# A hybrid decoder layer: a branch's results kept in SBUF, block sums on another engine and at other steps, stores and reloads traced later

## The chip, the cores and the metric

The kernel runs on one core of a Trainium2 chip. The metric is the device time of one execution in microseconds (us). The engines are PE (matrix products; PEld its weight loads), DVE (vector), ACT (scalar), POOL (GpSimd) and SP, whose queue issues nearly all DMAs here. Each engine works through its own queue in order.

## The reference

One layer with two token mixers on the same normalised input, for a prompt of 1040 tokens (16 learned meta tokens and 1024 of the sequence) and for 8 sample tokens. All of it is float32.

```python
proj = rmsnorm(h, norm_pre) @ w_in                   # 1024 -> 10 x 1024
q, fr, i_in, z_a, b_g, c_g, h_c, z_b, gate_a, gate_b = split(proj)
o = gated_linear_recurrence(silu(q), 1 - f, i_in, log f)   # 8 heads, 128x128 state
y_a = (norm(o) * silu(z_a)) @ w_a                    # branch A
u = c_g * h_c
y_b = (b_g * causal_conv3(u) * silu(z_b)) @ w_b      # branch B
merged = sigmoid(gate_a) * y_a + sigmoid(gate_b) * y_b
h = h + rmsnorm(merged @ w_o, norm_post)
```

It also returns the new recurrent states and the last two rows of u.

## The kernel before

**The products.** Tokens lie along the free dimension (1032 columns of a 128-row block), channels along partitions. A float32 product is made from three: both factors are split into a high and a low part, and `mm3` (L112) adds high x high, high x low and low x high. On top of that lies a Strassen scheme with seven products j = 0 to 6: `strassen` (L556) runs a list of *streams*, each a pair of 128-column blocks of weights against seven precomputed factors `s0` to `s6` of the right side (tiles `s0h`, `s0l` and so on). A stream has 14 *steps*, for each j two chunks of some 256 columns, 12 matmuls a step. There are 47 streams, numbered here from 0: 0 to 21 belong to the heads of branch A (with seven of the eight gate streams among them), 22 to 37 to the convolution (`u_pair` L670 and `b_pair` L730 in turn for 8 blocks), 38 to the last gate pair, 39 to 42 to y_a (`w_a`), 43 to 46 to y_b (`w_b`). In the windows below stream 38 starts at 990.60 us, 39 at 1019.60, 42 at 1094.10 and 45 at 1164.40; the windows are cut at the first product of a stream.

**The order.** The program is written out by hand (`manual_schedule`): an engine executes its instructions in the order in which the Python code issues ("traces") them. In each step `strassen` traces PE's 12 matmuls, then what was put off (`flush`: copies and evacuations of the step before), then the high part (ACT, L605) or the low part (DVE, L611) of the weights two products ahead, then whatever `at_step` (L861) has hung on that step's number. `add` (L587) forms two sums of weights for the next stream on POOL (L591 to L593), `low` a further one (L615). Held products are copied out of PSUM by ACT (L570); PE adds the next product onto the same bank, so it waits for that copy. Raw weights arrive in five slots `wq` by `load_quarter` (L93), four loads a stream.

**Between the branches.** The right side of y_a and y_b is the output of the recurrence (`oz_d`) or of the convolution (`ob_d`), kept in DRAM as 8 blocks of 128 x 1032. The seven factors need block sums: `block_sums(k, ...)` (L842) loads blocks k and k+4 into slots `f` and `k`, forms four differences of 128x516 in `s`, `f` and `k`, and stores them in `ta` or `tb` (three stores). The tags are slots of SBUF; a slot's new user waits until the last one is done. Branch A's four calls come out of `sample_steps` (L786), which computes the sample tokens of a head in 11 parts beside the convolution and is woven into 154 steps from step 350 on; branch B's four calls are hung on steps A0+6 to A0+36 (A0 = 546 is the first step of y_a, B0 = 602 that of y_b).

`exchange` (L864) replaces the factors while the products of the stream before still use the old ones: 14 units, one per half factor, each two loads of 258 KB into a raw slot, an ACT copy of 128x1032 (L90) and a subtraction of the same size (L91), on POOL for every third unit and on DVE for the others. Units are hung on steps A0-13 to A0+8 and B0-13 to B0+8, one every 1.65 steps. Branch A rotates through six raw slots, branch B through five; the reload of a slot is traced right behind the unit that frees it.

**The results.** The gates wait in DRAM (`ga_d`, `gb_d`). `gates_in` loads two blocks of them into `x` and `zs`; `y_pair` (L909) multiplies the product into the gate's slot; branch A's products are then stored in DRAM (`md`, L920), and in branch B `merged_in` loads them again (L906) to be added. After the streams the merged blocks are split and multiplied by `w_o`.

Of the kernel before, what the change touches and what calls it, by code (L numbers as in the profile page):

```python
# [19 lines left out]
HL = 524  # L20
HY = 516
# [11 lines left out]
def hybrid_step(ctx: ExitStack, tc: tile.TileContext,  # L33
# [728 lines left out]
    def context_out():  # L762
        for g in range(2):
            pt = hbank()
            for j in range(4):
                c = NEW + 18 * (4 * g + j)
                pe.transpose(pt[0:18, 128 * j:128 * j + 128], cx[:, c:c + 18], ident)
            nct = slot(("f", "s")[g], 512)
            act.copy(nct[0:18], pt[0:18])
            sync.dma_start(conv_p_out[0, 0][:, 512 * g:512 * g + 512], nct[0:2])  # L770
            sync.dma_start(conv_s_out[0].rearrange("b j d -> (b j) d")[:, 512 * g:512 * g + 512], nct[2:18])
# [13 lines left out]
    def sample_steps():  # L785
        loaded = sample_state(0)  # L786
        for m in range(8):
# [43 lines left out]
            if m >= 4:  # L831
                yield from block_sums(m - 4, oz_d, *sums_a)
# [9 lines left out]
    def block_sums(k, src, t12, t34):  # L842
        up, low, t = slot("f", NY), slot("k", NY), slot("s", NY)
        sync.dma_start(up, src[k])
        sync.dma_start(low, src[k + 4])
        yield
        yield
        less(t[:, L], up[:, R], up[:, L], pool)
        less(t[:, R], low[:, R], t[:, L], pool)
        yield  # L850
        sync.dma_start(t12[k], t)
        less(up[:, R], low[:, R], up[:, R], pool)
        less(low[:, L], low[:, L], t[:, R], pool)
        yield
        sync.dma_start(t34[k][:, L], up[:, R])
        sync.dma_start(t34[k][:, R], low[:, L])
        yield
# [3 lines left out]
    def at_step(g, f):  # L861
        hooks.setdefault(g, []).append(f)

    def exchange(g0, g1, base, sets, src, t12, t34, tags):  # L864


        of = lambda j, k: (src[k][:, L], src[k + 4][:, L], t12[k][:, R], t12[k][:, L], t34[k][:, L], t34[k][:, R],
                           src[k + 4][:, R])[j]
        raw = {}

        def load_unit(v):
            if v < 14:
                j, i = divmod(v, 2)
                raw[v] = slot(tags[v % len(tags)], NY)
                for q in range(2):
                    sync.dma_start(raw[v][:, HY * q:HY * q + HY], of(j, 2 * i + q))

        def unit(v):
            j, i = divmod(v, 2)
            if not i:  # L880
                sets[j] = factor(j)
            here = [[HL, 2], [1, HY]]
            split(raw[v].rearrange("p (q c) -> p q c", q=2), cap(sets[j][0], 2 * HL * i, here),
                  cap(sets[j][1], 2 * HL * i, here), pool if v % 3 == 2 else vec)
            load_unit(v + len(tags))

        for v in range(len(tags)):
            at_step(g0 + int(g1 * v), lambda v=v: load_unit(v))
        for v in range(14):
            at_step(base + 1 + int(1.65 * v), lambda v=v: unit(v))  # L890


    md = spilled("md")
    gated_ = {}
    merged = {}
    MERGED = ("v", "a", "ee", "s", "it", "u", "kt", "f")

    def gates_in(src, m):
        for r, tag in ((0, "x"), (1, "zs")):
            gated_[src is gb_d, m + r] = g = slot(tag, NY)  # L900
            sync.dma_start(g, src[m + r])

    def merged_in(m):
        for r in range(2):
            merged[m + r] = slot(MERGED[m + r], NY)
            sync.dma_start(merged[m + r], md[m + r])  # L906

    def y_pair(w, m, sets, second):
        def evac(r, h, c0, n, pt, s):  # L909
            ys = slice(HY * h + c0, HY * h + c0 + n)  # L910
            g = gated_[second, m + r][:, ys]
            vec.tensor_tensor(out=g, in0=added(pt, s), in1=g, op=ALU.mult)  # L912
            if second:
                t = merged[m + r][:, ys]
                vec.tensor_tensor(out=t, in0=t, in1=g, op=ALU.add)

        def end():
            if not second:
                for r in range(2):
                    sync.dma_start(md[m + r], gated_[second, m + r])  # L920

        return (w[0][:, 128 * m:128 * m + 128], w[0][:, 128 * m + 128:128 * m + 256]), chunks_of(HY), (), evac, end, sets
# [45 lines left out]
    exchange(A0 - 20, 1, A0 - 14, sets_a, oz_d, *sums_a, ("it", "u", "v", "a", "ee", "kt"))  # L968
    exchange(B0 - 20, 1, B0 - 14, sets_b, ob_d, *sums_b, ("it", "u", "kt", "f", "k"))
    at_step(A0 + 2, lambda: context_out())  # L970
    b_sums = (x for k in range(4) for x in block_sums(k, ob_d, *sums_b))
    for i in range(24):
        at_step(A0 + 6 + int(1.25 * i), lambda: next(b_sums, None))
    for i, m in enumerate((0, 2, 4, 6)):
        at_step(A0 - 11 + 14 * i, lambda m=m: gates_in(ga_d, m))
        at_step(B0 - 11 + 14 * i, lambda m=m: gates_in(gb_d, m))
        at_step(B0 - 8 + 14 * i, lambda m=m: merged_in(m))
# [199 lines left out]
    weave(stream, 14 * 11, sample_steps(), [1] * (8 * N_SAMPLE + 4 * 5))  # L1177
# [10 lines left out]
    wpost = slot("k", 1024)  # L1188
# [42 lines left out]
    xt, y, yl, ms = slot("v", 1024), slot("w", 1024), slot("a", 1024), small(2)  # L1231
# [50 lines left out]
```

## Time and profile before

| | |
|---|---|
| median of 3 runs | 1313.02 us (1312.26 to 1315.84) |
| the profiled execution | 1310.55 us, its span 1308.8 us |
| mean granted clock of PE | 0.989 |
| busy: PE, DVE, ACT, POOL | 1243.9, 940.0, 578.3, 504.7 us |
| moved by DMA | 148.85 MB |

Busy time is the sum of an engine's instructions; an engine that waits or issues DMAs is not busy. PEclk is the share of PE's full clock (2.4 GHz) that was granted in a stretch, its lower level 1.2 GHz. A row of waits says which engine's line waited for whom, how long in total, how often and the longest time. In a timeline, the brackets hold the idle time before an instruction and what ended it.

### The profile page before, as it was taken

The numbers are of one execution on the slowest core, as the hardware profiler recorded it, in microseconds if no ns is written. First come the engines' busy times: TensorE is split into PE (matmuls) and PEld (weight loads), VectorE is DVE, ScalarE is ACT, GpSimd is POOL, SyncE is SP. The second block draws the span as 40 slices with busy tenths as digits, with TensorE's granted clock in tenths as the row PEclk, the third lists the DMA queues.
The fourth block names the chain that finished last, engine by engine and source line by source line (L and its number), as shares of the span: only waits on it lengthen the run. The fifth ranks groups of instructions, "written<-read, shape, count | busy, mean of one in ns | idle before, by whom it ended". The sixth has DMA issues, their size and how long they took to land. (4 is left out here: it accounts for less than half of the span.)

```text
span 1308.8 us, 25416 instructions
## 1 busy us (share of the span) xinstructions
PE 1243.9 (95%) x9849; PEld 1203.7 (92%) x9849; DVE 940.0 (72%) x1520; ACT 578.3 (44%) x1364; POOL 504.7 (39%) x534
## 2 busy tenths in 40 slices
PE   6899999999999999999999999998998979899997
PEld 5799999999999999999999999898998979899876
DVE  5779596786959677695976788566865848979252
ACT  5455555455555545555443333333335514436031
POOL 5735242422423243242423444655744555520010
PEclk9899999999999999999999999999999989999999
DMA  6011212121121212112114354554337589753141
GB/s 221 9 46 55 61 57 82 59 74 59 58 67 55 82 55 75 58 58 68 55 60 139 106 146 114 162 168 126 113 115 266 197 278 357 255 200 125 49 163 56
DMA packets 162502, 148.85 MB, mean 114 GB/s; under 512 B 10353, under 2 KB 134362, under 8 KB 162382
## 3 DMA queue, kind: packets, MB, share of 16 engines
q1 hardware_dynamic: 161806, 145.14, 34.7%
q8 instruction: 77, 1.26, 0.4%
q0 software_dynamic: 576, 2.10, 0.4%
q14 instruction: 43, 0.35, 0.1%
HBM read 108.50 MB, written 38.67 MB: 112 GB/s over the span
## 5 line engine op out<-in xcount | busy, mean ns | idle before, releaser
L611 DVE TENSOR_TENSOR w<-wq,w 128x512 fp32r<-128x512 f32 x185 | 162.5, 878 | 66.3 <-ACT w L605 65.2
L605 ACT CAST w<-sm 128x512 fp32r<-128x512 f32 x141 | 87.3, 619 | 208.5 <-PE gb L116 134.0
L611 DVE TENSOR_TENSOR w<-sm,w 128x512 fp32r<-128x512 f32 x141 | 112.4, 797 | 48.7 <-ACT w L605 48.2
L591 POOL TENSOR_TENSOR sm<-wq 128x512 f32<-128x512 f32 x47 | 79.0, 1680 | 172.3 <-DVE w L611 153.8
L570 ACT COPY sc<-ga 128x256 f32<-128x256 f32 x216 | 80.1, 372 | 124.6 <-PE ga L116 104.9
L615 POOL TENSOR_TENSOR sm<-wq,sm 128x512 f32<-128x512 f32 x47 | 71.6, 1523 | 155.4 <-DVE w L611 112.9
L605 ACT CAST w<-wq 128x512 fp32r<-128x512 f32 x188 | 116.7, 622 | 29.4 <-PE ga L116 21.4
L114 PE MATMUL gb<-s1h,w 128*128 128x256 f32 (+3 forms) x376 | 109.0, 290 | 2.0 <-DVE sc L696 1.8
L114 PE MATMUL gb<-s3h,w 128*128 128x256 f32 (+3 forms) x376 | 109.2, 291 | 1.6 <-ACT w L605 1.1
L116 PE MATMUL gb<-s3h,w 128*128 128x256 f32 (+3 forms) x376 | 107.4, 286 | 3.2 <-DVE w L611 3.1
L114 PE MATMUL gb<-s6h,w 128*128 128x256 f32 (+3 forms) x376 | 108.3, 288 | 2.3 <-DVE f L288 1.5
L116 PE MATMUL gb<-s1h,w 128*128 128x256 f32 (+3 forms) x376 | 106.3, 283 | 2.8 <-DVE w L611 2.8
L115 PE MATMUL gb<-s3l,w 128*128 128x256 f32 (+3 forms) x376 | 107.0, 285 | 0.0
L115 PE MATMUL gb<-s6l,w 128*128 128x256 f32 (+3 forms) x376 | 106.5, 283 | 0.0
L115 PE MATMUL gb<-s1l,w 128*128 128x256 f32 (+3 forms) x376 | 106.2, 282 | 0.0
L116 PE MATMUL gb<-s6h,w 128*128 128x256 f32 (+3 forms) x376 | 106.0, 282 | 0.0
L288 DVE TENSOR_TENSOR sc<-gb,sc 128x256 f32<-128x256 f32 x192 | 80.5, 420 | 35.2 <-ACT sc L570 18.1
L593 POOL TENSOR_TENSOR sm<-wq 128x512 f32<-128x512 f32 x47 | 65.3, 1389 | 74.6 <-DVE w L611 73.5
L114 PE MATMUL ga<-s5h,w 128*128 128x256 f32 (+3 forms) x288 | 85.3, 296 | 8.5 <-ACT sc L570 8.0
L114 PE MATMUL ga<-s0h,w 128*128 128x256 f32 (+3 forms) x288 | 83.1, 288 | 1.1 <-DVE zs L327 1.1
L114 PE MATMUL ga<-s2h,w 128*128 128x256 f32 (+3 forms) x288 | 84.1, 292 | 0.0
L115 PE MATMUL ga<-s5l,w 128*128 128x256 f32 (+3 forms) x288 | 83.3, 289 | 0.4 <-DVE s5l L200 0.4
(677 smaller groups left out, 4487.8 us busy)
## 6 DMA issues: line engine op xcount, KB each, us to landing
wq<-in_w_in_dram SPq DMA_DIRECT2D x160, 256.0 KB
oz<-zs SPq DMA_DIRECT2D x16, 258.0 KB
ob<-zs SPq DMA_DIRECT2D x8, 516.0 KB
wq<-in_w_a_dram SPq DMA_DIRECT2D x16, 256.0 KB
wq<-in_w_b_dram SPq DMA_DIRECT2D x16, 256.0 KB
wq<-in_w_o_dram SPq DMA_DIRECT2D x16, 256.0 KB
wq<-in_x_prompt_dram SPq DMA_DIRECT2D x16, 256.0 KB
out_dram<-w SPq DMA_DIRECT2D x16, 256.0 KB
```

The lines of the kernel that those rows point to most:

```text
L114: pe.matmul(pt, wh, xh, start=first, stop=False, skip_group_check=onto)
L115: pe.matmul(pt, wh, xl, start=False, stop=False, skip_group_check=onto)
L116: pe.matmul(pt, wl, xh, start=False, stop=last, skip_group_check=onto)
L288: vec.tensor_tensor(out=out, in0=pt, in1=s, op=ALU.add)
L570: act.copy(held[j][:, cols], o)
L591: pool.tensor_tensor(out=s3, in0=a11, in1=a21, op=ALU.subtract)
L593: pool.tensor_tensor(out=s2, in0=a21, in1=a11, op=ALU.subtract)
L605: act.copy(w[:, 0:512], source(i))
L611: (pool if j in pairs[p][2] else vec).tensor_tensor(out=w[:, 512:1024], in0=source(i), in1=w[:, 0:512].bitcast(F32), op=ALU.subtract)
L615: pool.tensor_tensor(out=s2, in0=raws[p, 0, 1], in1=s2, op=ALU.subtract)
```

## The change

Branch A's gates are loaded into the eight slots that will hold the merged blocks, `ee`, `f`, `s`, `k`, `v`, `a`, `it`, `u`, and the product stays there; `md`, its eight stores and its eight reloads are gone. Branch B's gates use `x` and `zs`. With fewer free slots, exchange A has five raw slots (`it`, `u`, `v`, `a`, `kt`) and exchange B three (`kt`, `x`, `zs`), and a reload is traced two steps behind the unit that frees its slot.

`block_sums` runs on DVE, one subtraction a step, the first three steps after the loads are traced, and its stores come a step or two after what they store. All eight calls are hung on steps: branch A's at 435, 450, 465 and 480, branch B's at 494, 505, 516 and 541 (A0-5). The first seven lie beside the convolution (streams 31 to 37), the eighth in stream 38. `sample_steps` no longer calls them, and its 88 parts are woven into 126 steps in place of 108 into 154. The last rows of the convolution leave from `x` and `zs`, eight steps later, and three later loads use other slots.

```diff
@@ -765,7 +765,7 @@
             for j in range(4):
                 c = NEW + 18 * (4 * g + j)
                 pe.transpose(pt[0:18, 128 * j:128 * j + 128], cx[:, c:c + 18], ident)
-            nct = slot(("f", "s")[g], 512)
+            nct = slot(("x", "zs")[g], 512)
             act.copy(nct[0:18], pt[0:18])
             sync.dma_start(conv_p_out[0, 0][:, 512 * g:512 * g + 512], nct[0:2])
             sync.dma_start(conv_s_out[0].rearrange("b j d -> (b j) d")[:, 512 * g:512 * g + 512], nct[2:18])
@@ -828,8 +828,6 @@
             sync.dma_start(oz_d[m][:].rearrange("p (h c) -> p h c", h=2)[:, :, 512:516],
                            smpz[:, 8 * m:8 * m + 8].rearrange("p (h c) -> p h c", h=2))
             yield
-            if m >= 4:
-                yield from block_sums(m - 4, oz_d, *sums_a)
 
 
 
@@ -839,18 +837,22 @@
     sums_a, sums_b = sums_of("ta"), sums_of("tb")
     L, R = slice(0, HY), slice(HY, NY)
 
-    def block_sums(k, src, t12, t34):
-        up, low, t = slot("f", NY), slot("k", NY), slot("s", NY)
+    def block_sums(k, src, t12, t34, tags):
+        up, low, t = (slot(tag, NY) for tag in tags)
         sync.dma_start(up, src[k])
         sync.dma_start(low, src[k + 4])
         yield
         yield
-        less(t[:, L], up[:, R], up[:, L], pool)
-        less(t[:, R], low[:, R], t[:, L], pool)
-        yield
+        yield
+        less(t[:, L], up[:, R], up[:, L], vec)
+        yield
+        less(t[:, R], low[:, R], t[:, L], vec)
+        yield
+        less(up[:, R], low[:, R], up[:, R], vec)
+        yield
+        less(low[:, L], low[:, L], t[:, R], vec)
         sync.dma_start(t12[k], t)
-        less(up[:, R], low[:, R], up[:, R], pool)
-        less(low[:, L], low[:, L], t[:, R], pool)
+        yield
         yield
         sync.dma_start(t34[k][:, L], up[:, R])
         sync.dma_start(t34[k][:, R], low[:, L])
@@ -861,65 +863,57 @@
     def at_step(g, f):
         hooks.setdefault(g, []).append(f)
 
-    def exchange(g0, g1, base, sets, src, t12, t34, tags):
+    def exchange(g0, base, sets, src, t12, t34, tags):
 
 
         of = lambda j, k: (src[k][:, L], src[k + 4][:, L], t12[k][:, R], t12[k][:, L], t34[k][:, L], t34[k][:, R],
                            src[k + 4][:, R])[j]
-        raw = {}
+        raw = []
 
         def load_unit(v):
-            if v < 14:
-                j, i = divmod(v, 2)
-                raw[v] = slot(tags[v % len(tags)], NY)
-                for q in range(2):
-                    sync.dma_start(raw[v][:, HY * q:HY * q + HY], of(j, 2 * i + q))
+            j, i = divmod(v, 2)
+            if v < len(tags):
+                raw.append(slot(tags[v], NY))
+            for q in range(2):
+                sync.dma_start(raw[v % len(tags)][:, HY * q:HY * q + HY], of(j, 2 * i + q))
 
         def unit(v):
             j, i = divmod(v, 2)
             if not i:
                 sets[j] = factor(j)
             here = [[HL, 2], [1, HY]]
-            split(raw[v].rearrange("p (q c) -> p q c", q=2), cap(sets[j][0], 2 * HL * i, here),
+            split(raw[v % len(tags)].rearrange("p (q c) -> p q c", q=2), cap(sets[j][0], 2 * HL * i, here),
                   cap(sets[j][1], 2 * HL * i, here), pool if v % 3 == 2 else vec)
-            load_unit(v + len(tags))
-
-        for v in range(len(tags)):
-            at_step(g0 + int(g1 * v), lambda v=v: load_unit(v))
+
+        when = lambda v: base + 1 + int(1.65 * v)
         for v in range(14):
-            at_step(base + 1 + int(1.65 * v), lambda v=v: unit(v))
-
-
-    md = spilled("md")
-    gated_ = {}
-    merged = {}
-    MERGED = ("v", "a", "ee", "s", "it", "u", "kt", "f")
-
-    def gates_in(src, m):
-        for r, tag in ((0, "x"), (1, "zs")):
-            gated_[src is gb_d, m + r] = g = slot(tag, NY)
-            sync.dma_start(g, src[m + r])
-
-    def merged_in(m):
-        for r in range(2):
-            merged[m + r] = slot(MERGED[m + r], NY)
-            sync.dma_start(merged[m + r], md[m + r])
+            at_step(g0 + v if v < len(tags) else when(v - len(tags)) + 2, lambda v=v: load_unit(v))
+            at_step(when(v), lambda v=v: unit(v))
+
+
+    merged, gates_b = {}, {}
+    MERGED = ("ee", "f", "s", "k", "v", "a", "it", "u")
+
+    def gates_in(m):
+        for i in (m, m + 1):
+            merged[i] = slot(MERGED[i], NY)
+            sync.dma_start(merged[i], ga_d[i])
+
+    def gates_in_b(m):
+        for i, tag in ((m, "x"), (m + 1, "zs")):
+            gates_b[i] = slot(tag, NY)
+            sync.dma_start(gates_b[i], gb_d[i])
 
     def y_pair(w, m, sets, second):
         def evac(r, h, c0, n, pt, s):
             ys = slice(HY * h + c0, HY * h + c0 + n)
-            g = gated_[second, m + r][:, ys]
+            t = merged[m + r][:, ys]
+            g = gates_b[m + r][:, ys] if second else t
             vec.tensor_tensor(out=g, in0=added(pt, s), in1=g, op=ALU.mult)
             if second:
-                t = merged[m + r][:, ys]
                 vec.tensor_tensor(out=t, in0=t, in1=g, op=ALU.add)
 
-        def end():
-            if not second:
-                for r in range(2):
-                    sync.dma_start(md[m + r], gated_[second, m + r])
-
-        return (w[0][:, 128 * m:128 * m + 128], w[0][:, 128 * m + 128:128 * m + 256]), chunks_of(HY), (), evac, end, sets
+        return (w[0][:, 128 * m:128 * m + 128], w[0][:, 128 * m + 128:128 * m + 256]), chunks_of(HY), (), evac, lambda: None, sets
 
 
     gp, wo = {}, {}
@@ -965,16 +959,22 @@
     sets_a, sets_b = {}, {}
     stream_of += [y_pair(w_a, m, sets_a, False) for m in (0, 2, 4, 6)]
     stream_of += [y_pair(w_b, m, sets_b, True) for m in (0, 2, 4, 6)]
-    exchange(A0 - 20, 1, A0 - 14, sets_a, oz_d, *sums_a, ("it", "u", "v", "a", "ee", "kt"))
-    exchange(B0 - 20, 1, B0 - 14, sets_b, ob_d, *sums_b, ("it", "u", "kt", "f", "k"))
-    at_step(A0 + 2, lambda: context_out())
-    b_sums = (x for k in range(4) for x in block_sums(k, ob_d, *sums_b))
-    for i in range(24):
-        at_step(A0 + 6 + int(1.25 * i), lambda: next(b_sums, None))
+    exchange(A0 - 20, A0 - 14, sets_a, oz_d, *sums_a, ("it", "u", "v", "a", "kt"))
+    exchange(B0 - 20, B0 - 14, sets_b, ob_d, *sums_b, ("kt", "x", "zs"))
+    at_step(A0 + 10, lambda: context_out())
+
+    def at_steps(g, side):
+        for i in range(9):
+            at_step(g + i, lambda: next(side, None))
+
+
+    S0 = 14 * 25
+    for k in range(4):
+        at_steps(S0 + 15 * (k + 5) + 10, block_sums(k, oz_d, *sums_a, ("f", "k", "s")))
+        at_steps((494, 505, 516, A0 - 5)[k], block_sums(k, ob_d, *sums_b, ("f", "k", "s") if k < 3 else ("x", "zs", "x")))
     for i, m in enumerate((0, 2, 4, 6)):
-        at_step(A0 - 11 + 14 * i, lambda m=m: gates_in(ga_d, m))
-        at_step(B0 - 11 + 14 * i, lambda m=m: gates_in(gb_d, m))
-        at_step(B0 - 8 + 14 * i, lambda m=m: merged_in(m))
+        at_step(A0 - 11 + 14 * i, lambda m=m: gates_in(m))
+        at_step(B0 - (4 if i else 11) + 14 * i, lambda m=m: gates_in_b(m))
     for k, g in enumerate((3, 6, 9)):
         at_step(B0 + 42 + g, lambda k=k: (out_parts(k, 0), out_parts(k, 1)))
     stream = strassen(stream_of, hooks)
@@ -1174,7 +1174,7 @@
     ordered.enter_context(tc.manual_schedule())
     qz = slot("kt", 256)
     pool.memset(qz, 0.0)
-    weave(stream, 14 * 11, sample_steps(), [1] * (8 * N_SAMPLE + 4 * 5))
+    weave(stream, 14 * 9, sample_steps(), [1] * (8 * N_SAMPLE))
     drain(stream)
     ordered.close()
 
...
```

## Rows read from the trace of the kernel before

**Rows 1.** Windows: stretch, its us; busy us of PE, PEld, DVE, ACT, POOL; PEclk, DMA share, GB/s.

```profile
702.40:832.10 129.70, 128.22 (x1105) 125.13 (x1104) 99.98 (x164) 46.86 (x111) 60.62 (x73) 1.00 0.45 131
832.10:906.40 74.30, 65.50 (x544) 62.60 (x543) 51.10 (x87) 24.53 (x57) 40.00 (x47) 1.00 0.43 136
906.40:990.60 84.20, 82.55 (x693) 81.62 (x692) 60.34 (x100) 30.58 (x67) 45.98 (x47) 1.00 0.49 155
990.60:1019.60 29.00, 22.97 (x171) 22.76 (x170) 16.34 (x21) 15.43 (x27) 10.93 (x6) 0.88 0.72 235
1019.60:1094.10 74.50, 65.35 (x515) 64.50 (x514) 49.11 (x68) 25.28 (x49) 43.43 (x29) 0.93 0.76 259
1094.10:1117.90 23.80, 21.93 (x171) 21.72 (x170) 20.69 (x22) 13.73 (x21) 13.20 (x8) 0.93 1.00 363
1117.90:1143.60 25.70, 21.42 (x170) 20.39 (x170) 25.32 (x33) 12.01 (x19) 13.21 (x7) 1.00 0.75 258
1143.60:1164.40 20.80, 20.42 (x171) 20.21 (x170) 17.68 (x35) 6.49 (x14) 5.22 (x4) 1.00 0.52 180
1164.40:1184.50 20.10, 20.10 (x170) 20.10 (x170) 15.05 (x30) 6.49 (x14) 5.19 (x4) 1.00 0.46 158
```

**Rows 2.** PE's waits, 832 to 1185 us: total us, times, longest us.

```profile
PE h L114 <- ACT sc L570: 8.2, 3, 7.1
```

**Rows 3.** ACT's waits, 832 to 1185 us.

```profile
ACT w L605 <- POOL sm L593: 28.7, 4, 14.1
...
ACT sc L570 <- DMA gb<-sc: 6.9, 1, 6.9
```

**Rows 4.** Timeline of POOL: start us, us, instruction, idle before it.

```profile
829.73 1.30 POOL L219 TENSOR_TENSOR s<-f 128x516 f32<-128x516 f32 x1 [0.59 <-DMA f<-oz]
...
871.99 1.30 POOL L219 TENSOR_TENSOR s<-f 128x516 f32<-128x516 f32 x1 [7.24 <-DMA f<-oz]
...
877.60 2.29 POOL L591 TENSOR_TENSOR sm<-wq 128x512 f32<-128x512 f32 x1
```

**Rows 5.** POOL's waits, 700 to 1185 us.

```profile
POOL s L219 <- DMA f<-ob: 13.4, 3, 8.4
POOL s L219 <- DMA f<-oz: 8.2, 3, 7.2
```

**Rows 6.** The chain that ended last, in order of time: start us, us, what.

```profile
1067.93 1.17 POOL s L219
...
1077.93 0.58 PE h L114
...
1102.07 6.52 DMA u<-tb
...
1108.61 5.57 DMA v<-md
```

**Rows 7.** SP's waits, 980 to 1180 us.

```profile
SPq L851 <- POOL s L219: 21.7, 4, 7.6
```

**Rows 8.** DMA issues, 980 to 1180 us: how many, KB each.

```profile
md<-x SPq DMA_DIRECT2D x4, 516.0 KB
```

**Rows 9.** Timeline of DVE, 870 to 875.5 us.

```profile
870.78 0.69 DVE L611 TENSOR_TENSOR w<-sm,w 128x512 fp32r<-128x512 f32 x1 [1.98 <-ACT w L605]
...
874.74 1.74 DVE L611 TENSOR_TENSOR w<-wq,w 128x512 fp32r<-128x512 f32 x1
```

**Rows 10.** Timeline of SP: issues of block loads for branch A's sums.

```profile
825.74 0.60 SPq L844 DMA_DIRECT2D f<-oz  x1
...
866.01 0.43 SPq L844 DMA_DIRECT2D f<-oz  x1
```

**Rows 11.** Timeline of all engines, units of exchange A, 993.5 to 1002.7 us.

```profile
993.72 1.05 ACT L90 CAST s0h<-it 128x1032 fp32r<-128x1032 f32 x1 [1.09 <-PE ga L116]
...
996.06 1.72 SPq L876 DMA_DIRECT2D it<-ta  x2
...
1000.12 2.46 POOL L91 TENSOR_TENSOR s1l<-v,s1h 128x1032 fp32r<-128x1032 f32 x1 [6.05 <-ACT s1h L90]
```

More of the change, by code (lines that the diff above doesn't have):

```diff
@@ L1185, in hybrid_step @@
         out_parts(k, which)
-    wpost = slot("k", 1024)
+    wpost = slot("kt", 1024)
     sync.dma_start(wpost[:, 0:1024], norm_post.broadcast_to([128, 1024]))
@@ L1228, in hybrid_step @@
         residual(128, y, ms, xt, y_prompt[0][128 * t:128 * t + 128, :])
-    xt, y, yl, ms = slot("v", 1024), slot("w", 1024), slot("a", 1024), small(2)
+    xt, y, yl, ms = slot("ee", 1024), slot("w", 1024), slot("f", 1024), small(2)
     sync.dma_start(xt[0:8, 0:1024], xs)
```

## The prediction

> **What bounds the kernel now.** I read the table of windows first. The main products are cut into streams of 14 steps, and each window is one stream or several. When TensorE never stops, a stream takes 20.1 us: in the last window of the group PE is busy for all 20.10 us [rows 1]. Whatever a window takes beyond 20.1 us a stream was lost to waiting, or to the lower granted clock that follows a wait. The six streams from 702 to 832 lose 129.7 - 120.6 = 9.1 us, 1.5 us each; the three from 832 lose 74.3 - 60.3 = 14.0; the four from 906 lose 84.2 - 80.4 = 3.8. Then come stream 38 (990.6) with 8.9, the branch-A streams 39 to 41 with 74.5 - 60.3 = 14.2, and the branch-B streams 42 to 44 with 3.7, 5.6 and 0.7, 10.0 together [rows 1]. The reachable pool is so 14.0 + 3.8 + 8.9 + 14.2 + 10.0 = 50.9 us, of which the change touches every part.
>
> PE's own waits name ACT's copy of held products as the last to come: 8.2 us into the bank `h` alone, 7.1 at the longest [rows 2]. So next I ask what ACT waits for. It waits for POOL: 28.7 us behind L593, 14.1 at the longest; and once, 6.9 us, for a DMA, the store of a gate block out of the slot that ACT wants [rows 3]. POOL's timeline shows why. The block sums of branch A stand in its queue: it waits 7.24 us for their load at 871.99, spends four times 1.3 us or more on them, and only at 877.60 gets to L591, the first of three operations that form the operands of the next stream [rows 4]. POOL waited 13.4 us for the loads of branch B's sums and 8.2 us for branch A's [rows 5]. The chain of waits runs through the same place from a sum at 1067.93 over POOL's L591 to L593 and ACT's copy to PE's restart at 1077.93 [rows 6]. The loss from 832 to 906 and most of that of streams 39 to 41 are thus one fault: an in-order engine stands before a load while work for PE waits behind it. SP has the same fault: it waited 21.7 us for POOL's first sums before storing them [rows 7], with the weight loads behind.
>
> **Part 1: branch B's sums leave the A streams.** Sixteen POOL operations, their waits and twenty DMAs go from steps 552 to 582 to steps 494 to 550. With them goes the wait that the chain shows, and the lower granted clock after it (0.93 over the three streams [rows 1]). The eight stores of products to `md` go as well, 516 KB each [rows 8], and so do the eight reloads. What is late next is the exchange's own subtractions, of which I leave 2.0 us over three streams. Gain 14.2 - 2.0 = 12, bounds 8 (6 us of lateness stay, as in stream 43) and 14.
>
> **Part 2: stream 38.** Its wait is a store stuck in a full queue of transfers [rows 3]. Reloads of exchange A are traced two steps later, so SP no longer stands before a fresh split ahead of the gate stores, and by step 540 two fewer units of 516 KB have been asked for. Against it, block 3 of branch B's sums puts loads of twice 516 KB at step 541. I take half of the loss away: 8.9 to 4.0, gain 4.9. Bounds: a gain of 8 if the store lands in time; a loss of 4 if the block's loads come in front of it (four transfers of 516 KB, 2.1 MB, take 5.8 us at the 363 GB/s of the fullest window [rows 1], of which a step of 1.44 us may be hidden).
>
> **Part 3: the sums beside the convolution, on DVE.** Without POOL's share the 14.0 us should fall to the common 1.5 a stream. What is added: 32 tensor operations on 128x516. DVE shows a 128x512 subtraction of two SBUF operands at 0.69 us alone and at 1.74 beside POOL's sum [rows 9]. DVE works 99.98 us in six streams, 16.7 each [rows 1]. Four operations every 15 steps add 4 x 0.69 x 14/15 = 2.6, so 19.3 of 20.1: full, but covered; if the cover goes they cost 2.6 a stream. I take 0.69, because the 1.74 is measured against the very POOL sums that go. And DVE now does the waiting. The first sum comes three steps, 4.3 us, after its load is traced; from issue to use the loads took 3.99 (825.74 to 829.73) and 5.98 us (866.01 to 871.99) [rows 4, 10]. So DVE may stand 0 to 1.7 us, and behind it queue the low halves of the weights (L611) and the evacuations, both read by PE; about a step of delay is absorbed. I put streams 31 to 33 at 2.2 us each (6.6, gain 7.4) and 34 to 37 at 1.5 each (6.0, loss 2.2): net gain 5. Bounds: 9 if DVE never makes PE wait; a loss of 8 if each of the seven blocks there waits 1.7 and pays 4 x 1.05 for the port, less the 3.4 us that DVE has free in a stream: 7 x 2.5 = 17 against the 9.
>
> The Trainium skill, "SBUF — State Buffer", section "Who interferes with whom", says that a VectorE operation with two SBUF inputs and a GpSimd one that reads SBUF exclude each other, the later one standing until the earlier ends. It speaks against this change, and the 1.74 us agrees; by it every sum that meets a POOL operation would cost about 0.69 + 1.3 = 2.0 us, an estimate, and this is the second rival below.
>
> **Part 4: exchange B on three slots instead of five.** A unit holds its slot for ACT's copy (1.05 us) and the subtraction, on POOL 2.46 us; on DVE the reload was issued 2.34 us after the copy began (993.72 to 996.06) [rows 11]. With 4.0 to 6.0 us for the load, a turn takes 6.3 to 8.3 us on DVE and 7.5 to 9.5 on POOL. The hooks allow 3 x 1.65 steps of 1.44 us, 7.1. Over 11/3 turns the loop is thus from 3 early to 9 late; I take 4 late, since the middle of the two ranges is 0.8 too slow a turn. Relief comes on the other side: `md` leaves the queue, which was at 1.00 of its share in stream 42 and stood in the chain with 6.52 us for a reload and 5.57 for `v<-md` [rows 1, 6]. The part of the loss that is DVE's own stays (25.32 us busy of 25.7 in stream 43 [rows 1]). I take 7.7 in place of 10.0: gain 2.3, bounds -9 and +8.
>
> By the Trainium skill, "DMA: Bandwidth & Descriptors", section "Anatomy of one DMA", a transfer of 516 KB takes about 2.0 + 1.2 = 3.2 us, an estimate; the rows of this case show more. By it the loop would never be late.
>
> **Edits costed at nothing.** Sample steps keep their pace (88 in 126 steps against 108 in 154), beside PE as in the first window, where a stream with such steps loses 1.5 us; without the cover that is what they would cost again. Changed slots for the context, the norm weights and the last tokens are free well before use. The in-place product of branch A is the same two DVE operations.
>
> **Sum.** 12 + 4.9 + 5 + 2.3 = 24.2. The profiled execution took 1310.55 us (span 1308.8), so its like would take 1286.4. It lies 2.5 below the median of the three runs, 1313.02; against that median the forecast is 1289.
>
> **Rivals.** (a) The three slots decide: ACT, in order, stands before loads in streams 42 to 44 and the loop is 9 us late. For: the 7.1 us a turn. Against: a queue freed of `md`. Then 1289 + 11 = 1300, chance 0.15. (b) The other side: DVE becomes the bound beside the convolution. If its sums cost 1.74 each, a stream needs 16.7 + 6.5 = 23.2 us, 3.1 over, on seven streams 22, plus eight waits of 1.7, 14: 36 us where 17.8 are lost now, so 23 worse than my part 3: 1312, no change. If stream 38 gains nothing either, 1317, slower. It decides from about 0.9 us a sum ((20.1 - 16.7) over the 4 x 14/15 = 3.73 operations of a stream), and turns the sign near 1.74. Against: POOL has less to do. Chances 0.07 and 0.06. (c) Better: POOL's silence speeds DVE everywhere, parts 1 to 3 reach their good bounds (2 + 3 + 4 more) and part 4 half of the way to its own (3 more): 1289 - 12 = 1277, chance 0.15. The change does what it says; a rival on that isn't needed.
>
> **How the numbers follow.** The forecast, 1281 to 1297, has 0.57. The range 1276 to 1305 takes in (a) and most of (c) and leaves out (b). About 0.3%, 4 us, is what a measurement of this kernel can tell from no change: faster 0.57 + 0.15 + 0.15 = 0.87, same 0.07, slower 0.06.
>
> **What would show it.** Right: no POOL wait behind a sum's load; streams 40 and 41 within 1 us of 20.1; DVE's 128x516 subtractions near 0.7 us; PE's wait behind ACT's copy in stream 41 gone. Wrong: DVE waits for `f<-oz` or `f<-ob` of over 3 us with PE idle behind them; sums near 1.75 us; ACT waiting for `kt`, `x` or `zs` in streams 42 and 43 by more than 10 us together; or PE still standing 6 us in stream 38.

## The result and the profile after

The changed kernel takes 1305.39 us (median of five runs, 1303.90 to 1305.84), the kernel before, in runs beside it, 1313.02. The ratio of the two means is 0.9932, interval 0.9917 to 0.9947: 7.6 us faster by the medians, some 9 by the ratio, where 24 were forecast, and just outside the range. The profiled executions, 1310.55 and 1305.40 us, differ by 5.2; 2.0 of these lie before stream 25 (it starts at 702.37 before, at 700.39 after), where the two programs do the same work. So the traces can place 3.2 us of the gain and no more.

The windows of the kernel after, cut as those of before (columns as in [rows 1], where each answers to its stage):

```profile
700.40:830.70 130.30, 127.90 (x1106) 125.12 (x1105) 99.46 (x164) 46.96 (x111) 60.61 (x73) 1.00 0.44 129
830.70:906.30 75.60, 68.50 (x563) 65.76 (x562) 62.01 (x103) 25.08 (x60) 33.28 (x42) 0.95 0.54 173
906.30:991.30 85.00, 82.67 (x675) 81.18 (x674) 60.36 (x112) 30.03 (x64) 30.02 (x36) 1.00 0.55 184
991.30:1018.80 27.50, 22.24 (x171) 22.02 (x170) 16.23 (x21) 15.33 (x27) 10.88 (x6) 0.88 0.89 305
1018.80:1045.30 26.50, 23.21 (x178) 22.47 (x178) 25.55 (x31) 13.29 (x23) 12.86 (x6) 0.94 0.65 208
1045.30:1085.60 40.30, 40.30 (x339) 40.30 (x338) 21.58 (x43) 12.61 (x26) 10.33 (x8) 1.00 0.46 152
1085.60:1112.20 26.60, 22.86 (x171) 22.39 (x170) 21.19 (x25) 13.84 (x21) 11.59 (x6) 0.91 0.60 189
1112.20:1138.70 26.50, 23.14 (x170) 22.44 (x170) 21.99 (x29) 11.92 (x19) 12.20 (x6) 0.90 0.61 198
```

In streams 40 and 41 (1045.30) PE never stops. All that these three streams still lose is in stream 39 (1018.80), where DVE is busy for 25.55 of 26.50 us. POOL works 7 us less from 831 to 906 than in [rows 1] (33.28 for 40.00) and 16 less from 906 to 991, yet the first of these stages got longer. In 42 and 43 the granted clock is now 0.91 and 0.90.

What a stage loses beyond 20.13 us a stream is the measure used below. It is worked out for every kernel from the first product of each stream in its trace; the forecast's value is its own term, reckoned from 20.1 us a stream.

```
streams    before  forecast  after    e1    e3    e4    e8    e9   e13
25-30         9.0        -     9.5   9.5   9.5   9.5   9.5   9.1   8.9
31-33        13.9      6.6    15.2  15.5  13.1  11.8  12.1   9.1   7.4
34-37         3.7      6.0     4.5  15.6   4.4   4.1   5.2   3.9   5.9
38            8.8      4.0     7.4   4.3   7.5   6.4   4.3   5.8   6.4
39-41        14.1      2.0     6.4   9.3   8.0   1.5   3.3   1.8   1.9
42-44         9.9      7.7    13.5  13.6   9.8  14.3   9.7   9.7   9.7
```

How far one profile can be trusted is seen from kernels that have the same program in a stage. After, e3, e4, e7, e8, e10 and e11 are alike up to stream 37, and lose 11.8 to 15.2 us in streams 31 to 33 (13.0 on the mean) and 3.4 to 5.2 (4.3) in 34 to 37: a difference of under 3 us between two profiles in 31 to 33 is no result. In streams 42 to 44, seven profiles of the same exchange B (after, e1, e2, e4 to e7) lose 13.2 to 14.3 us.

The waits of the kernel after from 832 to 1180 us (total us, times, longest), those of DVE:

```profile
DVE s L219 <- DMA f<-oz: 9.7, 2, 6.6
...
DVE s L219 <- DMA f<-ob: 2.2, 1, 2.2
```

and those of ACT, to be read beside [rows 3]:

```profile
ACT sc L570 <- DMA gb<-sc: 6.2, 1, 6.2
...
ACT s5h L90 <- DMA zs<-tb: 4.6, 1, 4.6
ACT s2h L90 <- DMA x<-tb: 4.5, 1, 4.5
...
ACT s1h L90 <- DMA kt<-ob: 1.9, 1, 1.9
```

The 28.7 us behind POOL's L593 are gone. The wait for the gate store has stayed, and the signs are mixed: all four that the prediction named for being right are there (no sum in POOL's waits, 40 and 41 at 20.13 us, 0.70 us for most of the subtractions, PE's wait in stream 41 gone), but of those for being wrong two are there as well, DVE standing over 3 us for a sum's load and ACT over 10 us for `zs`, `x` and `kt`, and nearly a third, PE standing 5.3 us in stream 38. The longest wait of DVE, in its timeline (start, duration, instruction, idle before it):

```profile
863.68 0.68 DVE L611 TENSOR_TENSOR w<-sm,w 128x512 fp32r<-128x512 f32 x1
870.98 0.70 DVE L219 TENSOR_TENSOR s<-f 128x516 f32<-128x516 f32 x1 [6.62 <-DMA f<-oz]
872.23 0.70 DVE L219 TENSOR_TENSOR s<-k,s 128x516 f32<-128x516 f32 x1 [0.55 <-DMA k<-oz]
872.84 0.69 DVE L611 TENSOR_TENSOR w<-wq,w 128x512 fp32r<-128x512 f32 x1
```

SP issued that load at 863.32, so it took 7.7 us to its use. Behind it stands L611, which PE wants: PE is idle for 2.81 us until 873.58.

```profile
873.58 0.39 PE L116 MATMUL ga<-s5h,w 128*128 128x256 f32 x1 [2.81 <-DVE w L611]
```

### The profile page after: what moved, and what is told of

Read it like the earlier page. It is cut to its first block, busy times and chain, and to the rows that moved or that the text cites. A ratio compares the mean times of both kernels' runs of the same rounds, so it can differ in the third digit from the quotient of the medians.

```text
span 1303.6 us, 25383 instructions
## 1 busy us (share of the span) xinstructions
PE 1245.4 (96%) x9849; PEld 1205.6 (92%) x9849; DVE 944.1 (72%) x1552; ACT 579.2 (44%) x1364; POOL 460.9 (35%) x502
## 2 busy tenths in 40 slices
DMA packets 160199, 140.40 MB, mean 108 GB/s; under 512 B 10098, under 2 KB 134107, under 8 KB 160079
## 5 line engine op out<-in xcount | busy, mean ns | idle before, releaser
L611 DVE TENSOR_TENSOR w<-wq,w 128x512 fp32r<-128x512 f32 x185 | 160.5, 868 | 65.2 <-ACT w L605 62.5
L615 POOL TENSOR_TENSOR sm<-wq,sm 128x512 f32<-128x512 f32 x47 | 72.1, 1534 | 181.7 <-DVE w L611 146.3
L611 DVE TENSOR_TENSOR w<-sm,w 128x512 fp32r<-128x512 f32 x141 | 107.3, 761 | 30.9 <-ACT w L605 30.4
L593 POOL TENSOR_TENSOR sm<-wq 128x512 f32<-128x512 f32 x47 | 64.9, 1382 | 89.3 <-DVE w L611 87.4
L114 PE MATMUL ga<-s5h,w 128*128 128x256 f32 (+3 forms) x288 | 84.9, 295 | 5.8 <-ACT sc L570 5.3
L116 PE MATMUL ga<-s5h,w 128*128 128x256 f32 (+3 forms) x288 | 82.7, 287 | 2.8 <-DVE w L611 2.8
```

The source lines that it names most:

```text
L114: pe.matmul(pt, wh, xh, start=first, stop=False, skip_group_check=onto)
L116: pe.matmul(pt, wl, xh, start=False, stop=last, skip_group_check=onto)
L593: pool.tensor_tensor(out=s2, in0=a21, in1=a11, op=ALU.subtract)
L611: (pool if j in pairs[p][2] else vec).tensor_tensor(out=w[:, 512:1024], in0=source(i), in1=w[:, 0:512].bitcast(F32), op=ALU.subtract)
L615: pool.tensor_tensor(out=s2, in0=raws[p, 0, 1], in1=s2, op=ALU.subtract)
```

## The experiments

All edits are to the kernel after, unless an entry names another. In its numbering the block sums are lines 840 to 858, the exchange lines 866 to 891.

**e1: the sums on POOL, at their new steps.**

```
-        less(t[:, L], up[:, R], up[:, L], vec)
+        less(t[:, L], up[:, R], up[:, L], pool)
...
```

> The changed kernel with its sixteen plus sixteen subtractions of the block sums back on POOL, at the new steps. In the changed kernel streams 31 to 33 lose 15.2 us beyond 20.1 a stream, 34 to 37 lose 4.5. Theory 1 (an in-order engine that stands before a late load is what costs, whichever engine it is): POOL now stands there, the operands of the next stream come late as before; streams 31 to 37 lose 16 to 26 us, total 1303 to 1312. Theory 2 (DVE's capacity is what costs: 32 operations of 0.69 us): with DVE relieved, streams 31 to 37 lose under 13 us, total 1297 to 1301.

Measured: 1318.75 us, ratio 1.0051 (1.0034 to 1.0068), slower than the kernel before. POOL's waits from 830 to 1040 us:

```profile
POOL s L219 <- DMA f<-oz: 21.1, 4, 8.4
...
POOL s L219 <- DMA f<-ob: 7.0, 1, 7.0
```

and ACT's for POOL in the same stretch:

```profile
ACT w L605 <- POOL sm L593: 9.4, 2, 5.9
ACT w L605 <- POOL wq L592: 8.5, 1, 8.5
```

The time and the 31.1 us lost in streams 31 to 37 lie above theory 1's ranges, and on its side: having the sums on DVE instead of POOL is worth 13 us at these steps, 11 of them in streams 34 to 37. Both engines stop for the same loads, POOL for 28.1 us, DVE, in its list above, for 11.9; and a POOL that stands keeps back the next stream's operands, which ACT's two rows show.

**e2: eight steps, not three, from the loads of branch A's blocks to their first subtraction.**

```
-        yield
-        yield
-        yield
+        for _ in range(lead):
+            yield
...
```

> The changed kernel with branch A's four block sums begun eight steps behind their loads in place of three; everything else as it is. Theory 1 (DVE standing before the load, 9.7 us over two of the four blocks): that wait falls below 2 us, stream 32 (26.2 us) comes down to 21 to 23, total 1300 to 1302. Theory 2 (capacity): the same operations are only moved by five steps, streams 31 to 34 keep within 2 us of their 96.5 us, total 1304 to 1307.

Measured: 1304.11 us, 0.9938 (0.9921 to 0.9954). DVE's list has no wait for `f<-oz` any more, and stream 32 takes 22.0 us instead of 26.2. But seven profiles without this edit have stream 32 at 23.0 to 26.4 us, 34 to 37 lose 5.7 for 4.5, and the total moves by 1.3 us in the medians and not at all in the ratios (0.9932 after). The wait was real; what it cost does not show in the time.

**e3: both exchanges' reloads traced right behind the unit that frees the slot.**

```
-            at_step(g0 + v if v < len(tags) else when(v - len(tags)) + 2, lambda v=v: load_unit(v))
-            at_step(when(v), lambda v=v: unit(v))
+            if v < len(tags):
+                at_step(g0 + v, lambda v=v: load_unit(v))
+            at_step(when(v), lambda v=v: (unit(v), v + len(tags) < 14 and load_unit(v + len(tags))))
```

> The changed kernel with the reloads of both exchanges traced right behind the unit that frees the slot, as in the kernel before, in place of two steps later. Theory 3 (in branch B the turn of a slot decides, and the two steps are part of it, because a weight load that waits for its slot stands in SP's queue ahead of the reload): ACT's waits for kt, x and zs in streams 42 and 43, 11.9 us together, fall below 6, streams 42 to 44 lose 8 to 10 us in place of 13.5. Rival (three slots are too few by the load's own time, wherever it is traced): they lose 12 to 15. Beside it, SP now stands before fresh splits in stream 38 again: stream 38 loses 7 to 10 us where it loses 7.3, and total is 1300 to 1306 by theory 3, 1304 to 1309 by the rival.

Measured: 1304.27 us, 0.9939 (0.9923 to 0.9956). Streams 42 to 44 lose 9.8 instead of 13.5; exchange A's side gives some of that back (39 to 41: 8.0 for 6.4), and the total does not move clear of noise. The streams side with theory 3.

**e4: branch B's block 3 at 20 steps into branch A's streams, not 5 ahead of them.**

```
-        at_steps((494, 505, 516, A0 - 5)[k], ...
+        at_steps((494, 505, 516, A0 + 20)[k], ...
```

> The changed kernel with branch B's last block (loads, four subtractions, stores) moved from step 541 (A0-5) to step 566 (A0+20), into streams 40 and 41, which lose nothing. Theory 4 (stream 39's loss of 6.4 us is the work of that block on a DVE that has the exchange's subtractions to do): stream 39 loses 0 to 3 us, streams 40 and 41 stay below 1 us each, stream 38 loses 5 to 7.5, total 1299 to 1302. Rival (stream 39 is late because stream 38 was held up and the exchange with it): stream 39 loses 5 to 7 us still, total 1304 to 1306.

Measured: 1300.66 us, 0.9915 (0.9898 to 0.9931). Stream 39 takes 21.59 us instead of 26.54, as theory 4 had it.

**e5: the 32 subtractions left out; loads and stores stay.**

> A diagnosis: the changed kernel with the 32 subtractions of the block sums left out (the blocks are loaded and stored as they are, so nothing on DVE waits for those loads and the two branches' factors are not the sums). Theory 6 (most of what streams 31 to 33 lose has nothing to do with the sums, but with the sample steps' work beside the convolution's taps): they still lose 8 to 12 us together (11.8 to 15.2 with the subtractions). Rival (the sums cost it, as the prediction had it): they lose under 6 us, about 1.5 a stream. In stream 39 the loss falls from 6.4 to under 3 by theory 4.

Measured: one execution, profiled, 1294.8 us. Streams 31 to 33 still lose 11.2 us (11.8 to 15.2 with the subtractions), 34 to 37 only 1.2, 39 to 41 2.9.

**e6: the sample steps of the last three heads left out; the sums stay.**

> A diagnosis: the changed kernel with the sample steps of heads 5 to 7 left out (their states and outputs are not computed), the first five heads at the same pace; the block sums are untouched. Theory 6: streams 31 to 33 lose under 7 us together, and stream 33 under 3 in place of 4.8 to 6.1. Rival (the sums): they lose 11 us or more as before, stream 33 over 4.

Measured: one execution, profiled, 1292.6 us. The window of streams 31 to 33, of about the same 76 us:

```profile
830.00:906.00 76.00, 75.50 (x624) 74.87 (x624) 57.74 (x101) 28.20 (x60) 27.09 (x33) 1.00 0.48 162
```

PE is busy for 75.50 us of it, with all the sums there; 1.4 us are lost over the three streams. DVE waits for the loads of the sums here too:

```profile
DVE s L219 <- DMA k<-oz: 2.9, 2, 2.7
...
DVE s L219 <- DMA f<-oz: 2.6, 2, 2.0
```

So 31 to 33 lose their time where the sample steps are, not through the sums alone or the waits for their loads: without the subtractions 11 us are lost, without the sample steps 1.4. Both are single executions, but the gap is nearly three times what profiles of one program differ by.

**e7: e4, and the first pair of branch A's gates loaded 3 steps ahead of stream 39, not 11.**

```
-        at_step(A0 - 11 + 14 * i, lambda m=m: gates_in(m))
+        at_step(A0 - (11 if i else 3) + 14 * i, lambda m=m: gates_in(m))
```

> Beside e4 (block 3 of branch B at step 566) the first two gate blocks of branch A, 516 KB each, are loaded at step 543 (A0-3) in place of 535 (A0-11). Theory 5 (in stream 38 ACT waits for the store of a gate block that stands in the queue of transfers behind these loads): stream 38 loses 2 to 4.5 us in place of e4's 6.4, total 1297 to 1299.5. Rival (the exchange's own reloads fill the queue): stream 38 loses 5.5 to 7, total 1300 to 1301.

Measured: 1302.85 us, 0.9924 (0.9899 to 0.9950). Stream 38 loses 1.9 for e4's 6.4, and 39 to 41 lose 9.3 for 1.5: stream 38 does as theory 5 says, the total fits neither. The wait stands in ACT's list from 1010 to 1045 us, a stream later:

```profile
ACT sc L570 <- DMA gb<-sc: 5.7, 1, 5.7
```

**e8: e4, and exchange B's reloads right behind the unit** (exchange A keeps its two steps).

> Beside e4, the reloads of exchange B alone are traced right behind the unit (branch A's stay two steps later). Theory 3: streams 42 to 44 lose 8.5 to 11 us in place of e4's 14.3, the rest as in e4, total 1295 to 1298. Rival (e3's gain in branch B came from a calmer start): they lose 12.5 to 15, total 1299 to 1302.

Measured: 1296.24 us, 0.9870 (0.9844 to 0.9895), theory 3's range. Streams 42 to 44 lose 9.7 (9.7 in e9, e11, e13 and e14 too, which keep this edit), and ACT's list from 1080 to 1145 us now has no wait for a load above 2.1 us:

```profile
...
ACT s6h L90 <- DMA x<-ob: 2.1, 1, 2.1
ACT s2h L90 <- DMA zs<-tb: 1.9, 1, 1.9
ACT s1h L90 <- DMA kt<-ob: 1.6, 1, 1.6
ACT s2h L90 <- DMA x<-tb: 1.0, 1, 1.0
```

**e9: e8, and the sample steps at 14 steps a head, begun five empty parts (some six steps) later.**

```
-    weave(stream, 14 * 9, sample_steps(), [1] * (8 * N_SAMPLE))
+    weave(stream, 118, offset(), [1] * (5 + 8 * N_SAMPLE))
```

> Beside e8, the sample steps are given a pace of 14 steps a head and start five parts later, so that a head's three large DVE operations always fall on steps 8 to 11 of a stream and never beside the convolution's taps (steps 0 to 3 of every odd stream); the work is the same. Theory 6, sharpened (it is the meeting of the two that costs, in streams 25, 31 and 33): streams 31 to 33 lose under 7 us in place of 12.1, streams 25 to 30 lose 5 to 8 in place of 9.5, total 1288 to 1292. Rival (the amount of the sample steps' work costs, wherever it falls): the losses of streams 25 to 33 stay within 3 us of their 21.6, total 1294 to 1298.

Measured: 1290.95 us, 0.9826 (0.9808 to 0.9844), the fastest with e13. Stream 33 falls from 24.9 to 20.5 us; 32, at 25.8, stays within the 23.0 to 26.4 of the seven profiles. Streams 31 to 33 lose 9.1 us, between theory and rival. The edit changes the rate as well as the place: the last head's last evacuation (L825) ends at 890 us instead of 907, before the middle of stream 33. So it shows that a stream with little sample work left in it loses little, as e6 does, and not that the place within a stream decides.

**e10: e8, and exchange B starts on five filled slots before it goes round on three.**

> Beside e8, exchange B starts with five raw slots filled (the second buffers of x and zs too) and turns through three from its sixth unit on; branch B's first gates are loaded five steps later, into the two that come free. Theory 3 (the turn of a slot decides): with two units more in hand streams 42 to 44 lose 4 to 8 us in place of 9.7, total 1291 to 1295. Rival (what is left there is DVE's and POOL's own work): they lose 9 to 11, total 1295 to 1298.

Measured: 1295.77 us, 0.9868 (0.9851 to 0.9884); 42 to 44 lose 9.5 us for e8's 9.7. The window from 1083 to 1140 us:

```profile
1083.00:1140.00 57.00, 50.51 (x398) 49.26 (x398) 53.20 (x69) 28.20 (x45) 25.40 (x13) 0.97 0.56 173
```

DVE is busy for 53.20 of 57 us while PE works 50.51. Once the reloads come in time, two more slots buy nothing, and DVE is what remains. Not all of that is work, though. Two of DVE's operations here:

```profile
1101.14 3.44 DVE L91 TENSOR_TENSOR s3l<-x,s3h 128x1032 fp32r<-128x1032 f32 x1
...
1117.55 2.33 DVE L920 TENSOR_TENSOR x<-sc,x 128x260 f32<-128x260 f32 x1
```

The same operations take 1.22 and 0.43 us elsewhere in this window; these two lie beside POOL's L91 (1100.89 to 1103.49, 1117.15 to 1119.59). Twelve operations in the window, each beside one of POOL's, take some 16 us more in all than their like. In the kernel before it is twelve and 15 us in streams 42 and 43, so the change did not bring it; no run here takes POOL's share of the exchange away.

**e11: e8, and the first gates of branch A at 7 steps ahead.**

> Beside e8, the first two gate blocks of branch A are loaded at step 539 (A0-7) in place of 535. Theory 5 (the loads in front of the gate stores make ACT wait, and loads behind them do not): streams 38 to 41 lose 3 to 6 us together in place of 7.6 (e7, with step 543, moved ACT's wait from stream 38 to 39 and lost 11.2), total 1292 to 1296. Rival (wherever these 1 MB go, one of the gate stores stands behind them): they lose 7 to 11 together, total 1296 to 1300.

Measured: 1295.45 us, 0.9876 (0.9858 to 0.9895). Streams 38 to 41 lose 6.9 for 7.6 (stream 38 1.9 for 4.3, 39 to 41 5.0 for 3.3): no more than a run's spread.

**e12: e9 and e10 together.**

> e9 and e10 together. If both theories hold their gains add up, since they lie in different streams: 5 us and more in streams 25 to 33 and 3 us in 42 to 44, total 1284 to 1290. If only one holds, 1289 to 1294; if neither, 1294 to 1298.

Measured: 1292.89 us, 0.9850 (0.9832 to 0.9868), not better than e9 alone.

**e13: e9 with the eight-step lead of e2.**

> This is e9 with the first subtraction of a block of branch A eight steps behind its loads instead of three. Theory 7: what is left in streams 31 and 32 of e9 (23.25 and 25.76 us, 8.7 us over two streams of 20.13) is the second in-order wait, DVE's for the loads of the sums (f<-oz, 5.1 us in two waits there), in front of the taps' writes: with the longer lead that wait falls under 1 us, stream 32 to 22.5 or less, the stage of streams 31 to 33 loses 3 to 6 us where e9 lost 9.1, and the time is 1285 to 1289 us. Rival (sample work): stream 32 is long because a sample group and DVE's exact products meet its taps wherever the sums stand; then the wait goes but stream 32 stays over 24.5 us and the time at 1290 or more.

Measured: 1290.94 us, 0.9835 (0.9822 to 0.9848), the time of e9. DVE's wait for the loads is gone and stream 32 falls from 25.8 to 22.3 us, as theory 7 had it. But 33 rises from 20.5 to 22.9 and 35 from 21.4 to 24.0; streams 31 to 37 lose 13.3 us, in e9 13.1. The total is the rival's: with the wait gone, the same sums five steps later cost as much in other streams, and why is not shown.

**e14: e13 with the first gates at 7 steps ahead.**

> This is e13 with the first pair of branch A's gates loaded 7 steps ahead of branch A's streams instead of 11. Theory: the wait of ACT for the gate store in stream 38 loses its turn to stream 39, as in e11 beside e8, where streams 38 to 41 lost 6.9 instead of 7.6 us; so the time is within 2 us of e13's. Rival: with block 3 of branch B and the sample steps gone from streams 38 and 39, the wait finds an empty place and 3 us or more are gained.

Measured: 1291.60 us, 0.9830 (0.9816 to 0.9843). Stream 38 loses 1.9 for 6.4 us, 39 to 41 lose 6.6 for 1.9. For the third time the wait is handed on to the next stream. No version beats e9 and e13.

## Why the prediction was wrong

Of the four parts only the first worked by its mechanism, and it fell short. The step that missed most in the two profiles is in part 3: the loss beside the convolution was put down to POOL's sums, and it is there without them. That the time came within 0.4 us of the range is no merit: its upper end was there for rival (a), which brought 3.6 of its 9 us.

**Part 1, the A streams: mechanism right, size off by a third.** The loss fell by 7.7 us, not 12, just under the lower bound of 8. PE's wait behind ACT in stream 41 is gone, and 40 and 41 lose nothing at all. The step that failed is "What is late next is the exchange's own subtractions, of which I leave 2.0 us over three streams". Block 3 of branch B's sums runs amid that exchange's units for `s3` and `s4`, and DVE, which does most of the units, does these sums too. DVE's timeline in stream 39 of the kernel after:

```profile
1022.34 2.92 DVE L611 TENSOR_TENSOR w<-sm,w 128x512 fp32r<-128x512 f32 x1
1025.19 1.22 DVE L91 TENSOR_TENSOR s4l<-kt,s4h 128x1032 fp32r<-128x1032 f32 x1
1026.33 1.78 DVE L219 TENSOR_TENSOR zs<-zs,x 128x516 f32<-128x516 f32 x1
1028.04 0.41 DVE L288 TENSOR_TENSOR sc<-gb,sc 128x256 f32<-128x256 f32 x1
1028.48 2.43 DVE L912 TENSOR_TENSOR ee<-sc,ee 128x256 f32<-128x256 f32 x1
```

The four sums take 3.85 us here (one of them the 1.78), and six operations that lie beside POOL's, three of them in these lines, take 8.5 us more than their like (5.8 in e4). With the block 25 steps later, where DVE is busy for only 21.58 of 40.30 us, the three streams lose 1.5 us (e4; 1.5 to 3.4 in e8, e9, e10, e12 and e13, which keep that edit), so the 2.0 would have been about right. The prediction counted this block's loads in stream 38 and nowhere its work in 39.

**Part 2, stream 38: the wait that was to shrink did not.** 8.8 became 7.4, not 4.0 (4.9 in e2, which has the same program there). The step that failed is "so SP no longer stands before a fresh split ahead of the gate stores". SP's wait for the split did go, but another, for a weight load whose slot POOL still reads, stands in its place. SP's longest wait from 990 to 1012 us, before and after:

```profile
SPq L876 <- DVE s0l L91: 7.2, 1, 7.2
```

```profile
SPq L96 <- POOL sm L615: 3.9, 1, 3.9
```

And the store that ACT wants is not late for SP's sake alone. Before, it goes out 13.8 us into the stream, and ACT's copy runs 6.3 us after that:

```profile
1004.44 0.39 SPq L757 DMA_DIRECT2D gb<-sc  x1
```

```profile
1010.78 0.37 ACT L570 COPY sc<-ga 128x256 f32<-128x256 f32 x1 [6.94 <-DMA gb<-sc]
```

After, it goes out 13.1 us into the stream, behind an issue of 2.02 us, and the copy runs 6.3 us later again:

```profile
1002.27 2.02 SPq L878 DMA_DIRECT2D u<-ta  x2
1004.39 0.38 SPq L757 DMA_DIRECT2D gb<-sc  x1
```

```profile
1010.65 0.37 ACT L570 COPY sc<-ga 128x256 f32<-128x256 f32 x1 [6.18 <-DMA gb<-sc]
```

So the 6.3 us from issue to use stayed. That the wait is "a store stuck in a full queue of transfers" fits, but the DMA share is 0.89 in this stream, 0.72 in [rows 1]: the queue got fuller, not emptier. Later gate loads take 4.5, 2.4 and 4.5 us out of stream 38 and put 7.8, 1.7 and 4.7 into 39 to 41 (e7, e11, e14).

**Part 3, the sums beside the convolution: the step that missed most.** It was to gain 5 and lost 2 in the two profiles; on the mean of the seven alike up to stream 37 it neither gained nor lost (17.3 us in 31 to 37 against 17.6). "Without POOL's share the 14.0 us should fall to the common 1.5 a stream" took the last wait in POOL's queue for the cause. POOL's share went and 15.2 us stayed, 13.0 on the mean. e5 and e6 show that it comes from the sample steps, which the prediction left at the 1.5 us a stream of the first window ("Edits costed at nothing"). With them streams 31 to 33 lose 11.2 us though no subtraction is done, without them 1.4 though all are. What in them does it was not told apart: DVE's work (PE's waits of over 1 us in this stage, with the subtractions and without, all end with a DVE operation), the chain through its engines, or their meeting the blocks' loads and stores, which e5 leaves in. For 34 to 37 the estimate held (4.5 for 6.0). The price of a subtraction was right: 27 of the 32 took 0.68 to 0.85 us, five 1.4 to 1.8. The wait on loads came out longer than its term, 7.7 us from issue to use against the 4.0 to 6.0 taken; but it is not what costs, since taking it away gains at most 1.3 us (e2) or nothing (e13), and in e6 it costs next to nothing.

By the Trainium skill, "SBUF — State Buffer", section "Who interferes with whom", a VectorE operation with two SBUF inputs and a GpSimd one that reads SBUF keep each other out. The trace agrees: the 2.92 and 1.78 us above lie beside POOL operations (L91 from 1022.28 to 1024.72, L615 from 1025.35 to 1027.57). The estimate of 2.0 us a sum that was drawn from it fits five sums of 32 at most, so rival (b) did not come; it is in the exchanges (e10) that DVE's operations grow so.

**Part 4, exchange B on three slots: sign wrong, inside its bounds.** 9.9 became 13.5 (forecast 7.7). The failed step is the turn of a slot, "6.3 to 8.3 us on DVE and 7.5 to 9.5 on POOL", set against "The hooks allow 3 x 1.65 steps of 1.44 us, 7.1". The 2.34 us from copy to reload in it were read from the kernel before, where the reload is traced right behind the unit. The two steps that the change adds, 2.9 us at 1.44 a step, are in no term, nor is SP's queue, in which a reload traced two steps later stands behind whatever SP was given before it. (A smaller slip: 0.8 us over 11/3 turns is 2.9 us late, not 4, and how 7.7 follows from that is not worked out.) One turn in the trace after, 12.4 us long, begins with ACT's copy out of `zs`; POOL then frees the slot at 1114.11 + 2.44 = 1116.55 us,

```profile
1112.98 1.05 ACT L90 CAST s4h<-zs 128x1032 fp32r<-128x1032 f32 x1
```

```profile
1114.11 2.44 POOL L91 TENSOR_TENSOR s4l<-zs,s4h 128x1032 fp32r<-128x1032 f32 x1 [5.58 <-ACT s4h L90]
1117.52 2.22 POOL L615 TENSOR_TENSOR sm<-wq,sm 128x512 f32<-128x512 f32 x1 [0.97 <-DVE w L611]
```

SP issues the reload 3.7 us later, right behind a weight load that goes out as POOL's L615 ends (1119.74),

```profile
1119.77 0.38 SPq L96 DMA_DIRECT2D wq<-in_w_b_dram  x1
1120.25 0.93 SPq L878 DMA_DIRECT2D zs<-tb  x2
```

and ACT, which takes its queue in order, stands until 1125.39, 5.1 us after that issue:

```profile
1125.39 1.06 ACT L90 CAST s5h<-zs 128x1032 fp32r<-128x1032 f32 x1 [4.60 <-DMA zs<-tb]
```

Rival (a) was right in kind: 3.6 us of its 9 came. Not the number of slots but the two steps make it: with three slots and the reload behind the unit the loss is 9.7 (e8), with five to start with 9.5 (e10). The 3.2 us a load that the prediction took from the Trainium skill, "DMA: Bandwidth & Descriptors", stand there in a section on transfers that GpSimd issues ("Anatomy of one DMA"). SP issues these, and the one above took 5.1 us.

**The sum.** Of the 24.2 us forecast, part 1 missed 4.3 us, part 2 3.5, part 3 7.1 and part 4 5.9, and streams 25 to 30 cost 0.5 more. That leaves 2.9; from stream 25 on the two profiled executions differ by 3.2. (Branch B's sums stood at steps 552 to 575 before, not to 582; nothing in the sum rests on it.) Parts 1 and 4 have a small mend: with both (e8) the kernel is 1.3% faster than the one before, with e9's edit as well 1.7%. The forecast was 1.8%, for a kernel without them.

## What to carry to other kernels

The wait that ends last names the work that is late, not the work that fills the engine: before counting a stage's loss as the gain of taking one part out, ask what the stage would lose with that part gone and the rest left, as leaving out each part in turn showed here. Later is not free for a reload: count the turn of a slot through the issuing queue as well, with what stands ahead of it there, and trace it where the slot comes free. And a block of moved work is counted where all of it runs, its arithmetic as well as its loads.

## What was not expected of the hardware

Four windows of the kernel after, around DVE's longest wait (columns as in [rows 1]):

```profile
862.00:866.00 4.00, 4.00 (x45) 3.66 (x45) 2.36 (x4) 1.54 (x4) 0.88 (x1) 1.00 1.07 285
866.00:870.00 4.00, 4.00 (x35) 4.00 (x35) 0.00 (x0) 1.07 (x3) 1.30 (x1) 1.00 0.85 272
870.00:874.00 4.00, 1.20 (x10) 0.99 (x9) 2.47 (x4) 0.90 (x2) 0.00 (x0) 1.00 0.52 186
874.00:878.00 4.00, 4.00 (x25) 4.00 (x24) 4.00 (x8) 0.36 (x2) 2.82 (x3) 0.66 0.61 237
```

The load of a block of 516 KB, 7.7 us from issue to use where 4.0 and 6.0 were seen before [rows 4, 10], was asked for in the first of them, with the DMA engines busy throughout (share 1.07). In stream 38 SP needed 2.02 us to issue two transfers (`u<-ta`) that elsewhere go out in 0.93. And a wait is paid for twice: in the last window PE is busy for all 4.00 us, but at a mean granted clock of 0.66, after the window in which it stood, and gets through 25 products; from 866 to 870 us, at 1.00, it got through 35. The changed kernel moves 140.40 MB instead of 148.85, 5.7% less, and its time fell by 0.6 to 0.7%.
